# A hybrid decoder layer: five gate products moved to an earlier call, and a gate-path block moved ahead of the sparse branch's last projection

## The chip, the cores and the metric

One core of one Trainium2 chip runs the whole layer. The metric is the device time of one execution in microseconds, the median of several. Of the engines, PE (TensorE) multiplies matrices, ACT (ScalarE) and DVE (VectorE) work elementwise, POOL (GpSimd) does a few special operations, and SP issues most of the transfers between memory and the chip.

## The reference

The layer mixes three branches over 1024 tokens of width 1024. All matrix products are in fp32.

```python
h = rms_norm(x, g_norm)
proj = h @ w_in                     # 1024 x 7912, split into the parts below
(q_a, k_a, v_a, q_i, k_i, w_i, z_a, c_q, c_kv, k_rope, z_b, q_m, z_m, gate_logits) = split(proj)
q_a = partial_rope(rms_norm(q_a), ...)              # the same for k_a, 8 heads of 64
o_a = dsa_attention(q_a, k_a, v_a, q_i, k_i, w_i)   # sparse: 256 keys a query, chosen by an indexer
o_b = causal_attention(q_b, k_b, v_b)               # dense: q_b, k_b, v_b from c_q, c_kv, k_rope
o_m = cross_attention(q_m, mem)                     # 4 heads, 256 memory tokens
ys = [o_a * silu(z_a), o_b * silu(z_b), o_m * silu(z_m)]
branch = [ys[n] @ w_branch[n] for n in range(3)]
out = x + sum(sigmoid(gate_logits[n]) * branch[n] for n in range(3)) @ w_out
```

## The kernel before

**Products.** An fp32 product is three matmuls (`mm3`, lines 273 to 275): the high half of one side by the high half of the other, high by low, low by high. `wsplit` (line 239) makes the halves of a weight tile: ACT casts the raw tile to the high half (line 240), DVE subtracts it from the raw tile for the low half (line 243). `wload` (line 245) takes a raw buffer, has SP load it (line 257), and splits it. The halves of h, transposed, stay in hTh and hTl all the time.

**Stages.** The norm and the memory branch come first (to 240 us), then the dense branch with its eight heads (to 520), then the indexer (to 680). From 680 to 1023 the outputs of the memory and the dense branch are projected, and in between come the sparse branch's own projections: `qkv(p)` for the four pairs of heads p = 0 to 3, and `z_early(0, w)` for blocks w of the sparse branch's gate path z_a. The sparse attention itself (1023 to 1240) and the last projections (to 1400) follow. In the background of 680 to 1002 DVE and ACT search each row's 256th largest index score by bisection (tiles kd.. and ka.., `run_topk`); what is left of it runs between the other work.

**Fillers.** The gate products (tiles f, weights f_.., results fo) are independent of everything else in a stage; `Filler.run(n)` hands out n of them, three matmuls of 512 columns each. `attention()` (line 530) calls it at four places ahead of its loop, with the four numbers of the tuple: for the dense branch `PREB`, after the first pair's keys and values have been made (`pre[0]`, line 544), after the next load is taken up (`pre[1]`), after the key transposes `k_prep` (`pre[2]`; tile bkt, line 963) and after the queries (`pre[3]`, line 550).

**The order.** The kernel is written in program order, and a list scheduler then orders the instructions of each engine by what is ready. Each engine works through its list in order; a wait at its head holds all behind it. Tiles of one tag share a ring of buffers, and a tile waits until the one whose buffer it takes has been read for the last time.

**Around the change.** `qkv(p)` loads four weight tiles of 384 columns (a{p}w0 to a{p}w3, three transfers each) and then makes eight blocks of 128 tokens, 24 matmuls of 384 columns each. ACT copies each block out of the accumulator (line 1398); after each four blocks come the squares (line 1405), sums (line 1406), POOL's power (line 233), the rotary embedding (lines 422 to 427) and the scaling (lines 1420 to 1423). `scaled` for the second four blocks is kept back in `behind` until the next `catch_up()`. `z_early(0, w)` loads two weight tiles (in the trace z0w_0r and z0w_4r, 256 KB each, for every w) and makes 48 matmuls of 512 columns (tile z); its results go through line 1269 on ACT and line 1270 on DVE to memory. The raw tiles of qkv and of z share a ring of two buffers (`pool_raw = [2, 8, 768]`, line 1201), their halves rings of eight and seven. `NZG = 3`: the blocks w = 0, 1, 2 are made early, the fourth later. In the text z_1 and z_2 are the blocks w = 1 and w = 2, z2_0 and z2_4 the two weight tiles of z_2, and a_0, a_1 the first and the second four blocks of a qkv; r, h and l at a name's end are the raw tile, the high and the low half.

Of the kernel before, what the change touches and what calls it, by code (L numbers as in the profile page):

```python
# [34 lines left out]
WSM = [1]  # L35
WSB = [1]
WSI = [1]
PREB = (0, 0, 0, 16)
PREA = (0, 0, 4, 4)
NFQ = 2  # L40
PFQ = 4
NZG = 3
# [57 lines left out]
def hybrid_kernel(  # L100
# [296 lines left out]
    def pool_filler(pool, jobs, bufs, banks):  # L397
        return Filler(half_loader(pool, bufs), lambda nm: pool.tile([P, 512], F32, tag="fo", name=nm, bufs=1), jobs, banks)

    def take_jobs(n, cnt):  # L400
        r = all_jobs[n][:cnt]
        del all_jobs[n][:cnt]
        return r
# [432 lines left out]
    with ExitStack() as ph:  # L836
# [176 lines left out]
        fp = ph.enter_context(tc.tile_pool(name="bfill", bufs=1, reuse_waits="tile"))  # L1013
        attention(kv_gen, k_prep, q_prep, scores, pv, pool_filler(fp, take_jobs("G", NFB), FW, FBB), PFB, PREB, GENB, LDJ)

# [260 lines left out]
    def z_early(n, w, zc, wpool, wk, bg, loaded=None):  # L1276
        get = z_part(n, w, zc, wpool, wk, loaded=loaded)
        for j in range(2):
            sz = get(j)
            nc.gpsimd.dma_start(s_z[w * P:(w + 1) * P, j * 512:(j + 1) * 512], sz)  # L1280
            bg(zi[0], 5.1)
        z_done.add((n, w))
# [52 lines left out]
    with w3s as ph:  # L1335
# [10 lines left out]
        def catch_up():  # L1346

            while behind:
                behind.pop()()
# [89 lines left out]
        def load_q(p, hh):  # L1439
            qs = st["q", p, hh] = hd.tile([P, NT, P], FR, tag="qs", name=f"aqs{p}_{hh}")  # L1440
            for j in range(2):
                nc.sync.dma_start(f(qs)[:, 4 * j:4 * j + 4, :],
                                  s_qa[p][j].rearrange("p (t h d) -> p t h d", t=4, h=2)[:, :, hh, :])
# [3 lines left out]
        def early(a, b):  # L1447
            for w in range(a, b):
                z_early(0, w, C_ZA, wpool, wk, run_topk)
                catch_up()  # L1450
# [5 lines left out]
        ys.close()  # L1456
        fp = hds.enter_context(tc.tile_pool(name="afill", bufs=1, side="right", reuse_waits="tile"))
        hd = hds.enter_context(tc.tile_pool(name="aheads", bufs=2, side="right", reuse_waits="tile"))
        early(1, 2)
        a3 = qkv(3)  # L1460
        with tc.issue_after(a3.ins):
            load_k(0)
            load_q(0, 0)
            load_q(0, 1)
        early(2, NZG)

    run_topk(None, 99)
    wkind[:] = [None, None]
# [188 lines left out]
```

## Time and profile before

| | |
|---|---|
| median of 3 runs | 1402.6 us (1394.78 to 1403.1) |
| profiled execution, its own time | 1402.0 us |
| its span in the trace | 1400.2 us |
| mean granted clock of PE | 0.994 of full speed |
| PE busy | 1358.3 us, 97% of the span |
| DVE busy | 957.9 us, 68% |
| ACT busy | 693.4 us, 50% |
| POOL busy | 213.7 us, 15% |
| share of PE in the chain of work that ended last | 67% |

Busy time says how full an engine is, not what the end waits for; where PE is as full as here, its idle stretches and what released it from them are to be looked for one by one. Times inside the trace count from the start of the span.

### The profile page before, as it was taken

What the parts mean: (1) busy time and instruction counts of PE and PEld (TensorE: products, weight loads), DVE (VectorE), ACT (ScalarE), POOL (GpSimd) and SP (SyncE); (2) the same over time, 40 slices, a digit from 0 to 9 for tenths busy, and PEclk for the clock granted to TensorE, in tenths of its full rate; (3) what the DMA queues carried; (4) which work ended last, traced back from release to release, by engine and by line L of the source; (5) the groups of instructions that cost most, each with busy time, mean ns of one, the idle gap of its engine ahead of it and who ended that gap; (6) DMA issues with size and microseconds to landing.
All of it is one profiled execution on the core that took longest, in us unless ns stands there. A gap on an engine that the chain in (4) does not pass through costs nothing.

```text
span 1400.2 us, 20838 instructions
## 1 busy us (share of the span) xinstructions
PE 1358.3 (97%) x7440; PEld 1167.8 (83%) x7440; DVE 957.9 (68%) x2346; ACT 693.4 (50%) x1520; POOL 213.7 (15%) x240
## 2 busy tenths in 40 slices
PE   7999999999999999999999999998999999999998
PEld 5998888878889888977898889788988888877787
DVE  5935445678888871388887777877768888858511
ACT  6635433256666652265665566443346666543200
POOL 3051003611101000000004102414220000004200
PEclk9999999999999999999999999999999999999999
DMA  7411222321111213011424741975351442267621
GB/s 248 141 46 53 78 62 69 108 82 38 57 50 38 64 44 114 15 39 37 131 74 167 239 113 47 224 167 146 111 182 52 129 136 54 69 195 232 197 98 67
DMA packets 154711, 147.45 MB, mean 105 GB/s; under 512 B 38000, under 2 KB 114800, under 8 KB 154608
## 3 DMA queue, kind: packets, MB, share of 16 engines
q1 hardware_dynamic: 147024, 123.58, 29.6%
q0 software_dynamic: 7008, 20.45, 4.9%
q10 hardware_dynamic: 576, 2.10, 0.4%
q8 instruction: 58, 0.95, 0.3%
q14 instruction: 45, 0.37, 0.1%
HBM read 99.43 MB, written 46.66 MB: 104 GB/s over the span
## 4 chain that ended last, share of the span: by engine, by line
PE 67%; DVE 13%; ACT 6%; DMA 4%; issue 4%; POOL 3%; SPq 1%; DVEq 0%; ACTq 0%; POOLq 0%
PE f L273 6%; PE f L274 5%; PE f L275 5%; DVE kdj L1039 3%; PE o L275 2%; PE o L273 2%; PE o L274 2%; PE br L273 2%; PE br L275 2%; PE br L274 2%; ACT kag L1045 2%; DVE idx L1233 1%; PE ixps L274 1%; PE ixps L275 1%; PE ixps L273 1%
## 5 line engine op out<-in xcount | busy, mean ns | idle before, releaser
L1045 ACT ACTIVATE kag<-idx,kaT 128x896 bf16<-128x896 f32 (+2 forms) x96 | 83.0, 865 | 43.5 <-DVE kaT L1066 34.2
L1039 DVE TENSOR_SCALAR_CACHE_REDUCE kdj<-idx,kdT 128x1024 bf16<-128x1024 f32 (+2 forms) x96 | 92.5, 964 | 1.1
L273 PE MATMUL f<-hTh,f_0h 128*128 128x512 f32 x184 | 78.8, 428 | 1.9 <-ACT fo L365 1.3
L273 PE MATMUL f<-hTh,f_1h 128*128 128x512 f32 x184 | 76.3, 415 | 0.0
L274 PE MATMUL f<-hTl,f_1h 128*128 128x512 f32 x184 | 74.4, 404 | 0.0
L275 PE MATMUL f<-hTh,f_0l 128*128 128x512 f32 x184 | 74.1, 403 | 0.0
L275 PE MATMUL f<-hTh,f_1l 128*128 128x512 f32 x184 | 73.9, 402 | 0.0
L274 PE MATMUL f<-hTl,f_0h 128*128 128x512 f32 x184 | 73.5, 400 | 0.0
L1588 POOL TENSOR_TENSOR ac<-ac,tg 128x512 f32<-128x512 f32 x16 | 24.1, 1520 | 257.6 <-DVE tg L1586 250.7
L1627 DVE TENSOR_TENSOR xr<-o,xr 128x512 f32<-128x512 f32 x16 | 11.1, 691 | 62.4 <-PE o L275 62.3
L365 ACT ACTIVATE fo<-f 128x512 f32<-128x512 f32 x48 | 28.8, 600 | 38.5 <-PE f L275 34.6
L1227 ACT ACTIVATE irl<-is 128x512 f32<-128x512 f32 (+1 forms) x80 | 37.8, 527 | 15.6 <-DVE idx L1233 11.9
L1233 DVE SCALAR_TENSOR_TENSOR idx<-irl,wi,idx 128x1024 f32<-128x1024 f32 (+5 forms) x42 | 40.3, 960 | 2.5 <-ACT irl L1227 0.8
L273 PEld LDWEIGHTS f<-hTh,f_0h 128*128 128x128 f32 x184 | 34.9, 190 | 8.2 <-ACT fo L365 3.1
L275 PEld LDWEIGHTS f<-hTh,f_0l 128*128 128x128 f32 x184 | 34.9, 190 | 6.8
L275 PEld LDWEIGHTS f<-hTh,f_1l 128*128 128x128 f32 x184 | 34.8, 189 | 6.0
L274 PEld LDWEIGHTS f<-hTl,f_1h 128*128 128x128 f32 x184 | 34.9, 190 | 4.3
L273 PEld LDWEIGHTS f<-hTh,f_1h 128*128 128x128 f32 x184 | 34.8, 189 | 4.1
L274 PEld LDWEIGHTS f<-hTl,f_0h 128*128 128x128 f32 x184 | 35.1, 191 | 3.6
L1225 PE MATMUL is<-kih,iqT 128*128 128x512 f32 (+1 forms) x80 | 30.1, 381 | 2.7 <-ACT irl L1227 2.4
L1174 DVE TENSOR_SCALAR wi<-ixps 128x8 f32<-128x8 f32 x8 | 1.3, 167 | 42.0 <-ACT xi L1172 42.0
L1226 PE MATMUL is<-kil,iqT 128*128 128x512 f32 (+1 forms) x80 | 27.5, 354 | 0.0
(1246 smaller groups left out, 4767.8 us busy)
## 6 DMA issues: line engine op xcount, KB each, us to landing
s_tg<-fo SPq DMA_DIRECT2D x48, 256.0 KB, 2.1
tg<-s_tg SPq DMA_DIRECT2D x48, 256.0 KB, 4.6
f_0r<-in_w_in_dram SPq DMA_DIRECT2D x23, 256.0 KB, 3.0
f_1r<-in_w_in_dram SPq DMA_DIRECT2D x23, 256.0 KB, 3.0
xx<-in_x_dram SPq DMA_DIRECT2D x8, 512.0 KB, 6.9
osb<-s_o SPq DMA_DIRECT2D x16, 256.0 KB, 3.4
s_acc<-ab POOLq DMA_DIRECT2D x16, 256.0 KB, 5.0
s_acc<-am POOLq DMA_DIRECT2D x16, 256.0 KB, 6.4
```

Source lines behind the costliest of these rows:

```text
L273: nc.tensor.matmul(ps, ah, bh, start=start, stop=False)
L274: nc.tensor.matmul(ps, ah, bl, start=False, stop=False)
L275: nc.tensor.matmul(ps, al, bh, start=False, stop=stop)
L365: nc.scalar.activation(o, ps, AF.Tanh, scale=0.5)
L1039: nc.vector.tensor_scalar(out=junk, in0=idx[t], scalar1=T[:, i:i + 1], scalar2=0.0, op0=ALU.is_ge, op1=ALU.add, accum_out=cnt[:, i:i + 1])
L1045: nc.scalar.activation(junk, idx[t], AF.Sign, bias=T[:, i:i + 1], accum_out=cnt[:, i:i + 1])
L1225: nc.tensor.matmul(sp[:, 0:w], q_, kih[:, k0:k0 + w], start=True, stop=False)
L1226: nc.tensor.matmul(sp[:, 0:w], q_, kil[:, k0:k0 + w], start=False, stop=True)
L1227: nc.scalar.activation(rl[:, k0:k0 + m], sp[:, 0:m], AF.Relu)
L1233: i_ = nc.vector.scalar_tensor_tensor(out=acc[:, 0:n], in0=rl[:, 0:n], scalar=wc, in1=acc[:, 0:n], op0=ALU.mult, op1=ALU.add)
L1588: nc.gpsimd.tensor_tensor(ac, ac, tg, op=ALU.add)
L1627: nc.vector.tensor_tensor(xr, ps, xr, op=ALU.add)
```

## The change

Two edits. The first moves numbers within the tuple that sets how many gate products go where ahead of the dense branch's loop: of the sixteen after the queries, five are asked for ahead of the key transposes. The second makes z_2 ahead of `qkv(3)` instead of behind it, so that nothing of the gate path lies between `qkv(3)` and the sparse attention; in its old place only `catch_up()` remains, which emits the scaling of the last four blocks.

```diff
-PREB = (0, 0, 0, 16)
+PREB = (0, 5, 0, 11)
...
-        early(1, 2)
+        early(1, NZG)
         a3 = qkv(3)
         with tc.issue_after(a3.ins):
             load_k(0)
             load_q(0, 0)
             load_q(0, 1)
-        early(2, NZG)
+        catch_up()
```

PE ahead of the dense branch's first key transposes, in the program as built. f_5_0 is the gate product in question, kv the keys and values of the first pair; the transposes (bkt) follow some twenty rows later.

```order
 L274 MATMUL kv_4_2965<-ukv0l,ckvh_1951 128x256
 L275 MATMUL kv_4_2965<-ukv0h,ckvl_1952 128x256
-L273 MATMUL f_5_0_3067<-hTh_0_142,f_5_1h 128x512
-L274 MATMUL f_5_0_3067<-hTl_0_158,f_5_1h 128x512
-L275 MATMUL f_5_0_3067<-hTh_0_142,f_5_1l 128x512
+L273 MATMUL f_5_0_3042<-hTh_0_142,f_5_1h 128x512
+L274 MATMUL f_5_0_3042<-hTl_0_158,f_5_1h 128x512
+L275 MATMUL f_5_0_3042<-hTh_0_142,f_5_1l 128x512
 L273 MATMUL kv_6_2993<-ukv0h,ckvh_1949 128x256
 L274 MATMUL kv_6_2993<-ukv0l,ckvh_1949 128x256
```

The three last matmuls of f_5_0 stand where they stood; the buffer has another number. The same holds for the other 21 of that product and for all instructions of the other engines up to the second edit.

SP, from z_1's two weight tiles on. The two added rows are z_2's; they were issued before behind the sparse attention's first keys and queries (akd, aqs).

```order
 L257 DMA z0w_0r<-in_w_in_dram 128x4x128
 L257 DMA z0w_4r<-in_w_in_dram 128x4x128
+L257 DMA z0w_0r<-in_w_in_dram 128x4x128
+L257 DMA z0w_4r<-in_w_in_dram 128x4x128
 L257 DMA a3w0r<-in_w_in_dram 128x2x128 x3
 L257 DMA a3w1r<-in_w_in_dram 128x2x128 x3
 L257 DMA a3w2r<-in_w_in_dram 128x2x128 x3
 L257 DMA a3w3r<-in_w_in_dram 128x2x128 x3
```

z_2's tiles now stand ahead of the four weight tiles of qkv(3), and the ring's two buffers go round in that order: a3w0 waits for z_2's first low half, a3w1 for a3w0's, a3w2 for a3w1's, and a3w3 for z_2's second.

DVE, behind the scaling of qkv(2)'s second four blocks (a_1qs), about 978 us in the trace before. idx, kdi, kdc and kds are top-k.

```order
 L1423 TENSOR_TENSOR a_1qs<-a_1xq,a_1qs 128x8x64
 L1114 TENSOR_SCALAR idx_6264<-kae_10461 128x896
-L243 TENSOR_TENSOR a3w3l<-a3w3r,a3w3h 128x768
+L243 TENSOR_TENSOR z0w_4l<-z0w_4r,z0w_4h 128x512
 L1074 TENSOR_SCALAR kdi_10501,kdc<-kds_10499 128x768
 L1116 TENSOR_TENSOR idx_6264<-idx_6264,cmask 128x128
```

Where the low half of qkv(3)'s fourth weight tile stood, there stands now that of z_2's second. z_2's first low half went up to the place behind z_1's second, ahead of the block sz and the next top-k row (kdj); a3w1's and a3w2's went down one and two places. On PE the 48 matmuls of z_2 stand between z_1 and qkv(3), and behind qkv(3) both blocks of the first gate job, 48 matmuls, come ahead of the first scores S, where one block with 24 stood.

## Rows read from the trace of the kernel before

**Rows 1.** The page, busy time of PE: us, share of the span, instructions.

```profile
PE 1358.3 (97%) x7440; PEld 1167.8 (83%) x7440; DVE 957.9 (68%) x2346; ACT 693.4 (50%) x1520; POOL 213.7 (15%) x240
```

**Rows 2.** Waits of PE, whole span: who waits <- for whom: total us, times, longest.

```profile
PE a L274 <- DVE a3w3l L243: 4.3, 1, 4.3
PE bkt L963 <- POOL xk L948: 2.5, 1, 2.5
...
PE f L273 <- ACT fo L365: 1.3, 3, 0.6
```

**Rows 3.** PE in order of time: start us, us, line, operation, out<-in, [idle before <-releaser].

```profile
960.60 0.40 PE L273 MATMUL z<-hTh,z0w_0h 128*128 128x512 f32 x1
...
971.57 0.39 PE L275 MATMUL z<-hTh,z0w_4l 128*128 128x512 f32 x1
971.80 0.34 PE L273 MATMUL a<-a3w0h,hTh 128*128 128x384 f32 x1
...
974.97 0.34 PE L273 MATMUL a<-a3w3h,hTh 128*128 128x384 f32 x1
979.57 0.69 PE L274 MATMUL a<-a3w3l,hTh 128*128 128x384 f32 x1 [4.27 <-DVE a3w3l L243]
...
983.90 0.47 PE L275 MATMUL a<-a3w1h,hTl 128*128 128x384 f32 x1
```

**Rows 4.** Stretches: us, PE busy, PEld, DVE, ACT, POOL, granted clock, DMA share, GB/s.

```profile
980.00:982.00 2.00, 2.00 (x8) 2.00 (x8) 2.00 (x7) 0.00 (x0) 0.25 (x1) 0.50 1.13 400
...
1030.00:1240.00 210.00, 205.89 (x1270) 175.06 (x1269) 173.18 (x493) 130.06 (x286) 0.00 (x0) 1.00 0.35 100
```

**Rows 5.** SP in order of time: weight loads issued before qkv(3).

```profile
925.25 0.37 SPq L257 DMA_DIRECT2D z0w_0r<-in_w_in_dram  x1
930.01 0.37 SPq L257 DMA_DIRECT2D z0w_4r<-in_w_in_dram  x1
932.14 1.39 SPq L257 DMA_DIRECT2D a3w0r<-in_w_in_dram  x3
...
964.86 1.39 SPq L257 DMA_DIRECT2D a3w2r<-in_w_in_dram  x3
```

**Rows 6.** ACT in order of time: casts that make the high halves.

```profile
930.77 0.62 ACT L240 CAST z0w_0h<-z0w_0r 128x512 fp32r<-128x512 f32 x1 [1.86 <-DMA z0w_0r<-in_w_in_dram]
...
933.01 0.62 ACT L240 CAST z0w_4h<-z0w_4r 128x512 fp32r<-128x512 f32 x1 [1.12 <-DMA z0w_4r<-in_w_in_dram]
...
968.55 0.84 ACT L240 CAST a3w2h<-a3w2r 128x768 fp32r<-128x768 f32 x1 [4.75 <-DMA a3w2r<-in_w_in_dram]
```

**Rows 7.** DVE in order of time: low halves, top-k and the last rows of qkv(2).

```profile
933.66 0.69 DVE L243 TENSOR_TENSOR z0w_4l<-z0w_4r,z0w_4h 128x512 fp32r<-128x512 f32 x1
...
934.87 0.61 DVE L1039 TENSOR_SCALAR_CACHE_REDUCE kdj<-idx,kdT 128x384 bf16<-128x384 f32 x1
...
963.89 0.93 DVE L243 TENSOR_TENSOR a3w0l<-a3w0r,a3w0h 128x768 fp32r<-128x768 f32 x1
...
969.95 0.69 DVE L1406 TENSOR_REDUCE a_1ss<-a_1sq 128x8 f32<-128x512 f32 x1 [2.19 <-ACT a_1sq L1405]
...
977.67 0.68 DVE L1423 TENSOR_TENSOR a_1qs<-a_1xq,a_1qs 128x512 fp32r<-128x512 f32 x1
...
978.57 0.95 DVE L243 TENSOR_TENSOR a3w3l<-a3w3r,a3w3h 128x768 fp32r<-128x768 f32 x1
```

**Rows 8.** PE (z, f, S), then DVE, in order of time at the head of the sparse attention.

```profile
1012.11 0.39 PE L273 MATMUL z<-hTh,z0w_0h 128*128 128x512 f32 x1
...
1023.27 0.39 PE L273 MATMUL f<-hTh,f_0h 128*128 128x512 f32 x1
...
1029.95 0.40 PE L1537 MATMUL a_3S<-akh,a_3qT 128*128 128x512 f32 x1
...
1023.29 0.69 DVE L1423 TENSOR_TENSOR a_1qs<-a_1xq,a_1qs 128x512 fp32r<-128x512 f32 x1 [1.83 <-ACT a_1qs L1422]
...
1025.23 1.29 DVE L1496 TENSOR_TENSOR akl<-akt,akh 128x512 fp32r<-128x512 f32 x2 [0.44 <-ACT akh L1495]
```

## The prediction

> **What bounds the kernel now.** I read the page first: PE is busy for 1358.3 of the 1400.2 us [rows 1], so the whole kernel is one queue of matmuls, and a change that only moves matmuls can win or lose no more than idle time and half-clock time of PE, 42 us in all. Then the table of PE's waits, longest first: it names where those us lie. Two of its rows bear on this change [rows 2]: the 4.3 us in which qkv(3), the last projection of the sparse branch, waits for the low half of its fourth weight tile (a3w3l), and the 2.5 us in which the first key transposes of the dense branch (bkt) wait for POOL's xk. The third row is a small wait for the eviction of a gate product, used below. Then PE in order of time around 972 us [rows 3]: z_1's 48 matmuls of 512 columns run 0.233 us apart (960.60 to 971.57), qkv(3) starts at 971.80 with 0.176 us a matmul, and its 20th matmul starts at 979.57 instead of 975.15. So 4.42 us are lost there. Behind it the clock is at its lower level: the granted clock is 0.50 in 980 to 982 [rows 4], and 14 matmuls from 979.57 to 983.90 take 4.33 us for 13 steps that cost 2.29 at 0.176: 2.04 us more. This stall costs 6.46 us in all.
>
> **Edit 1, the five gate products ahead of the key transposes: 0 us.** The tuple moves five of the sixteen steps to an earlier call, but the scheduler already had the products of that job ahead of the transposes. In the programs as built the instructions of PE, DVE, ACT, POOL and SP stand in the same order with the same waits until the second edit begins; only buffer numbers differ. What this edit might have covered, the 2.5 us before bkt [rows 2], stays.
>
> **Edit 2, z_2 ahead of qkv(3).** What it takes away: qkv(3) starts 48 x 0.233 = 11.2 us later on PE, so a3w3l, late by 4.4 us, is no longer what ends last. That is -6.46 us.
>
> What it adds is a new wait of the same kind. The raw weight ring has two buffers. Before, SP used them after z_1's two tiles (issues at 925.25 and 930.01) for a3w0 at 932.14 and a3w1, and the third, a3w2r, could go only at 964.86, when a3w0l had been made [rows 5]. Now z_2's two tiles take those two places. Their high halves are soon made on ACT, but the low half of the second, z2_4l, stands in DVE's order where a3w3l stood: behind a_1qs and one top-k row. That is the row at 978.57 [rows 7], long after the data has landed. PE needs it at the 15th matmul of z_2 (k = 4, the L275 product): 971.80 + 14 x 0.233 = 975.07.
>
> When is it made? First z2_0: issued at 932.14, where a3w0r was. z_1's tiles needed 5.5 us (925.25 to the cast at 930.77) and 3.0 us (930.01 to 933.01) to land [rows 5, 6]. I take 3.0, since the like of it has one transfer of this size just ahead of it and nothing large behind, and keep 5.5 as the upper bound. It lands at 935.1; by the steps of z_1's second tile the low half starts 0.65 us after the cast (933.01 to 933.66) and the next top-k row 1.21 us after that (933.66 to 934.87). So the top-k row that started at 934.87 starts at 935.14 + 0.65 + 1.21 = 937.0: DVE is 2.1 us late. From there DVE is full, then hands its results to POOL's power (a_0rr), ACT and back, in order, so the 2.1 us stay in the chain until a3w0l (963.89, now about 966.0). Behind that hangs SP's next issue (a3w1r now, in a3w2r's place), its landing 3.7 us later (964.86 to 968.55), ACT's cast, and behind that cast in ACT's order the square a_1sq, hence DVE's a_1ss (969.95), the power on POOL, a_1qs (977.67) [rows 5 to 7]. All of it 2.1 us late, so z2_4l starts at about 980.7; it has 512 columns, 0.69 us as z_1's [rows 7], and PE starts at 981.4. Lost: 981.4 - 975.07 = 6.3 us, and the half clock behind it as before, 2.04: +8.4 us. Bounds: with no lateness at all (some idle time of DVE swallows it) the loss is 4.2 + 2.0 = 6.2; with the landing of 5.5 us, 8.9 + 2.0 = 10.9.
>
> The Trainium skill (SBUF — State Buffer, "The DMA setup-cost knee") puts a transfer at about 2 us plus its bytes over 436 GB/s, so 2.6 us for these 256 KB. By that estimate DVE would be 1.7 us late instead of 2.1, and the sum would come out 0.4 us lower. The trace shows 3.0 and 5.5 for the same tile, and the sum goes by the trace.
>
> Is there a second stall at a3's own weights? a3w1r to a3w3r now go out one by one, each when a low half is done; a3w3r last, behind z2_4l at 981.4. With 3.7 us to land and the cast and low half behind top-k rows it is there by about 989. PE has 34 matmuls of z_2 left (7.9 us, and 2 for the half clock), so qkv(3) starts at 991.3 and wants a3w3l 3.3 us later. No stall; 5 us to spare. The loads behind it on SP (keys, queries, f_0's weights) are wanted after 1023, 40 us later.
>
> **The head of the sparse attention.** Before, z_2 lay between qkv(3)'s end (1012.11) and the gate products, and covered the normalisation of the last rows: a_1qs came 11.2 us after that end, the scores S 17.8 us after it [rows 8]. Now S of the first unit comes behind 48 gate matmuls, 16 key transposes and the queries: 11.2 us and about twice the 1.1 us that they took between 1023.27 and 1029.95, so 13.4 us behind qkv(3). The query copy on DVE stands behind a_1qs, two more akl (0.65 each), a weight split and takes 0.4: about 13.0. It just fits. Two small prices remain: the second gate block waits for the eviction of the first, at most the 0.6 us of such a wait [rows 2], I take 0.4; and 24 matmuls of filler (5.6 us) that used to lie under S and softmax are spent earlier, in a stretch that has only 4.1 us of idle PE in 210 [rows 4] and meets the old order again at the fifth gate job: 0 to 2 us, I take 0.3, since more gate products stand ready behind.
>
> **Sum.** -6.46 + 8.4 + 0.4 + 0.3 = +2.6 us on the profiled execution's 1402.0 us: 1404.6. That execution lies 0.6 us below the median of the runs (1402.6), so the forecast, rounded down for that z_1's gate on ACT no longer stands behind a late cast, is 1404.5.
>
> **Rivals.**
> (a) The stall goes away: z2_4l is made before 975.07. For it: ACT has the high half by about 938, and the data lies there for 40 us. Against it: DVE works in order, and what stands ahead needs the last rows of qkv(2), whose matmuls end at 960.60; even with no lateness the chain puts z2_4l at 978.6. Price: -6.46 + 0.7 = -5.8, 1396.
> (b) z_2's first tile lands as slowly as z_1's first, 5.5 us: DVE is 4.6 us late, the loss at this place 10.9 instead of 8.4, and the time 1407.
> (c) The other side, slower: the head of the sparse attention starves. The query copy waits for a chain through ACT, DVE and POOL that z_2 no longer covers; it has about 0.4 us to spare. Each us that it is later is a us of idle PE, and past some us the half clock adds 2 more: 2 to 8 us late gives 1407 to 1415. It is over 1% only if the chain is about 10 us later than I reckon; nothing in the rows is that long.
> (d) Edit 1 acts after all and takes bkt's wait away with its half clock: -2.5 - 2.0, so 1400 with the rest. Against it stands the identical order.
>
> **How the numbers follow.** Forecast (1402 to 1407) 0.62; (b) 0.13; (a) 0.10; (c) 0.09; (d) 0.03; something unseen 0.03. The range 1397 to 1410 leaves out (a), half of (c) and the unseen: 0.17. A measurement of this kernel can tell about 1% from no change (its three runs lie 0.6% apart). All that the edits touch, 6.5 us at one stall and 4.5 at the other, is under 1%, so faster has 0.01; slower needs the far end of (c): 0.03; within 1%: 0.96.
>
> **What would show it.** In the waits of PE after: no row for a3w3l; in its place z, L275, for z's second low half, about 6 us; bkt unchanged at 2.5; half clock from about 981 to 985 among z_2's matmuls. The DVE row of that low half directly behind a_1qs and idx at about 980.7, and the low half of z_2's first tile near 935.8. A wait of S or of a query transpose in the first unit under 1 us. I am wrong if z's second low half is made much earlier or PE waits for a3's weights too, and the sum is then off by the us in those two rows.

## The result and the profile after

The changed kernel takes 1409.3 us (1407.3 to 1411.2) beside 1400.8 us of the kernel before on the same chip (1394.8 to 1403.1): a ratio of 1.0063, with a 95% interval of 1.0046 to 1.0081. It is slower by 8.5 us, under 1%, where +2.6 was forecast. The time lies above the forecast's own range of 1402 to 1407 and 0.7 us inside the outer one, 1397 to 1410. The profiled execution took 1409.46 us (span 1407.7), 7.5 more than that of before.

Busy times on the page, as in [rows 1]:

```profile
PE 1360.6 (97%) x7440; PEld 1167.8 (83%) x7440; DVE 956.4 (68%) x2346; ACT 692.4 (49%) x1520; POOL 214.8 (15%) x240
```

The same work, 2.3 us more busy time of PE (matmuls at half clock count as busy) and 5 us more of idle time. PE's waits, longest first, as in [rows 2] (total us, times, longest):

```profile
PE z L275 <- DVE z0w_4l L243: 6.6, 1, 6.6
...
PE f L273 <- ACT fo L365: 2.8, 5, 0.9
...
PE a_2pt L462 <- DVE a_2p L519: 2.5, 2, 2.0
PE bkt L963 <- POOL xk L948: 2.5, 1, 2.5
```

The row for a3w3l is gone and a row for z_2's second low half stands in its place, 6.6 us long (6.3 were forecast). bkt waits as before. But there is a wait that the prediction did not have: a transpose of the attention's probabilities (a_2pt) waits 2.0 us for DVE, where the same row of the kernel before had 0.4 at most:

```profile
PE a_2pt L462 <- DVE a_2p L519: 0.9, 2, 0.4
```

PE at the first of these places, as in [rows 3], and the stretches around it, as in [rows 4] (the seventh figure, just ahead of the last two, is the granted clock):

```profile
971.78 0.39 PE L273 MATMUL z<-hTh,z0w_0h 128*128 128x512 f32 x1
...
974.81 0.40 PE L274 MATMUL z<-hTl,z0w_4h 128*128 128x512 f32 x1
981.85 0.80 PE L275 MATMUL z<-hTh,z0w_4l 128*128 128x512 f32 x1 [6.64 <-DVE z0w_4l L243]
982.44 0.63 PE L273 MATMUL z<-hTh,z0w_4h 128*128 128x512 f32 x1
...
986.71 0.48 PE L274 MATMUL z<-hTl,z0w_0h 128*128 128x512 f32 x1
```

```profile
978.00:980.00 2.00, 0.00 (x0) 0.00 (x0) 0.00 (x0) 0.45 (x1) 1.97 (x3) 1.00 0.35 131
980.00:982.00 2.00, 0.15 (x1) 0.15 (x1) 1.80 (x4) 2.00 (x4) 0.58 (x2) 0.52 0.35 131
...
984.00:986.00 2.00, 2.00 (x6) 1.52 (x6) 2.00 (x2) 0.00 (x0) 0.54 (x1) 0.50 0.93 269
...
988.00:990.00 2.00, 2.00 (x10) 1.65 (x9) 1.21 (x2) 1.75 (x3) 0.00 (x0) 1.00 0.88 184
...
1030.00:1240.00 210.00, 203.86 (x1230) 171.31 (x1228) 169.29 (x496) 124.05 (x274) 7.54 (x13) 0.99 0.35 101
```

z_2's 15th matmul was due at 974.81 + 0.23 = 975.04 and started at 981.85: 6.8 us. The ten steps from 982.44 to 986.71 have 0.427 us each where they want 0.233: granted clock 0.50, the lower level of 1.2 GHz; with the slower steps at either end that is 2.4 us. The last line is the other half of the result: of 210 us in the sparse attention PE is now idle 6.1, where it was 4.1 [rows 4].

Why z0w_4l came when it came: SP, ACT and DVE in order of time, as in [rows 5 to 7].

```profile
931.06 0.37 SPq L257 DMA_DIRECT2D z0w_0r<-in_w_in_dram  x1
934.38 0.37 SPq L257 DMA_DIRECT2D z0w_4r<-in_w_in_dram  x1
935.96 1.39 SPq L257 DMA_DIRECT2D a3w0r<-in_w_in_dram  x3
966.43 1.39 SPq L257 DMA_DIRECT2D a3w1r<-in_w_in_dram  x3
```

```profile
934.59 0.62 ACT L240 CAST z0w_0h<-z0w_0r 128x512 fp32r<-128x512 f32 x1 [0.97 <-DMA z0w_0r<-in_w_in_dram]
...
937.25 0.62 ACT L240 CAST z0w_4h<-z0w_4r 128x512 fp32r<-128x512 f32 x1 [1.54 <-DMA z0w_4r<-in_w_in_dram]
```

```profile
965.47 0.93 DVE L243 TENSOR_TENSOR a3w0l<-a3w0r,a3w0h 128x768 fp32r<-128x768 f32 x1
...
971.46 0.69 DVE L1406 TENSOR_REDUCE a_1ss<-a_1sq 128x8 f32<-128x512 f32 x1 [2.99 <-ACT a_1sq L1405]
...
980.20 0.69 DVE L1423 TENSOR_TENSOR a_1qs<-a_1xq,a_1qs 128x512 fp32r<-128x512 f32 x1 [2.39 <-ACT a_1qs L1422]
980.81 0.39 DVE L1114 TENSOR_SCALAR idx<-kae 128x896 bf16<-128x896 bf16 x1
981.11 0.68 DVE L243 TENSOR_TENSOR z0w_4l<-z0w_4r,z0w_4h 128x512 fp32r<-128x512 f32 x1
```

The tile is in SBUF and its high half is being made at 937.25. Its low half stands on DVE behind a_1qs and idx, as the order said, at 981.11: 44 us later. a3w0l is 1.6 us later than before (2.1 were forecast); a_1qs, with a wait for ACT of its own, is 2.5 later.

The head of the sparse attention, as in [rows 8]: the first scores on PE, and the copy of their queries on DVE.

```profile
1039.59 0.40 PE L275 MATMUL f<-hTh,f_1l 128*128 128x512 f32 x1
1039.82 0.40 PE L1537 MATMUL a_3S<-akh,a_3qT 128*128 128x512 f32 x1
```

```profile
1038.10 0.68 DVE L243 TENSOR_TENSOR f_1l<-f_1r,f_1h 128x512 fp32r<-128x512 f32 x1
1038.70 0.42 DVE L1523 CAST a_3qT<-a_3q 128x256 fp32r<-128x256 f32 x1
```

The queries are there 0.7 us ahead of S; S waits for nothing. What is lost is lost behind it. From the last score of the tile a_2 to the transpose of its probabilities, DVE and ACT need nearly the same time in both kernels: 1122.31 to 1126.87 before, 1130.66 to 1135.53 after. Before, 12 gate matmuls lie in between on PE (the last at 1126.45); after, 6, and then nothing is left that is ready. The kernel before, then the kernel after, PE in order of time:

```profile
1122.31 0.28 PE L1538 MATMUL a_2S<-akl,a_2qT 128*128 128x256 f32 x1
...
1126.45 0.39 PE L275 MATMUL f<-hTh,f_1l 128*128 128x512 f32 x1
1126.87 0.41 PE L462 MATMUL a_2pt<-ident,a_2p 128*128 128x128 f32 x2
```

```profile
1130.66 0.28 PE L1538 MATMUL a_2S<-akl,a_2qT 128*128 128x256 f32 x1
...
1133.11 0.40 PE L1538 MATMUL a_1S<-akl,a_1qT 128*128 128x512 f32 x1
1135.53 0.41 PE L462 MATMUL a_2pt<-ident,a_2p 128*128 128x128 f32 x2 [2.03 <-DVE a_2p L519]
...
1138.19 0.63 PE L275 MATMUL f<-hTh,f_0l 128*128 128x512 f32 x1
```

Behind this wait, too, the granted clock is at its lower level for a while:

```profile
1137.00:1139.00 2.00, 2.00 (x8) 1.50 (x7) 1.64 (x3) 1.20 (x3) 0.00 (x0) 0.52 0.46 165
1139.00:1141.00 2.00, 2.00 (x13) 1.96 (x12) 0.12 (x1) 0.00 (x0) 0.00 (x0) 0.63 0.00 0
```

**Where the time went, by stretches.** PE's timeline is cut at the 96 score products (line 1538). "Lost" is the length of a stretch less its matmuls at their usual step (median distance to the next: 0.23 us for 512 columns, 0.17 for 384, 0.12 for 256, 0.083 for 128), so it holds waits, half clock and the small gaps at each change of work. For z_1 to qkv(3) the steps are those of [rows 3]. The steps are rounded, so an entry holds to a few tenths. "1st to 16th" goes from the first score product to the start of the 17th, and so on by sixteens; "to last" ends where the 96th starts, and the last column where the last matmul starts. In the text the head is everything from the end of qkv(3) to the end of "to 48th". In brackets stands the number of gate matmuls f in the stretch. Before and after come first, the experiments of the next section below them.

| kernel | z_1 to end of qkv(3) | to 1st score | 1st to 16th | to 32nd | to 48th | to last | behind it, whole length |
|---|---|---|---|---|---|---|---|
| before | 6.6 | 0.5 (24) | 2.4 (54) | 4.2 (58) | 4.4 (62) | 9.6 (156) | 166.7 (30) |
| after | 9.3 | 1.2 (48) | 3.3 (49) | 5.2 (49) | 8.5 (53) | 9.5 (155) | 164.6 (30) |
| e1_preb | 7.5 | 0.4 (24) | 2.4 (54) | 4.1 (58) | 4.3 (62) | 9.5 (156) | 164.3 (30) |
| e2_z | 6.7 | 1.2 (48) | 3.4 (49) | 5.2 (49) | 8.4 (53) | 9.2 (155) | 163.2 (30) |
| e3_wz8 | 0.0 | 1.2 (48) | 3.5 (49) | 5.3 (49) | 7.0 (53) | 9.6 (155) | 160.7 (30) |
| e5_z3 | 7.9 | 1.1 (24) | 2.5 (54) | 4.2 (58) | 4.4 (62) | 9.6 (156) | 163.1 (30) |
| e10_late | 0.8 | 5.8 (24) | 2.3 (54) | 4.2 (58) | 4.4 (62) | 9.4 (156) | 164.1 (30) |
| e11_late_after | 1.8 | 1.9 (48) | 3.5 (49) | 5.3 (49) | 8.5 (53) | 9.5 (155) | 160.2 (30) |
| e12_prea | 7.5 | 0.9 (48) | 2.7 (54) | 4.8 (57) | 3.7 (61) | 9.4 (158) | 162.3 (6) |
| e16_prea_after | 8.6 | 1.4 (51) | 4.3 (53) | 4.7 (55) | 3.9 (61) | 9.4 (158) | 162.4 (6) |
| e18_66 | 4.2 | 1.2 (48) | 3.9 (49) | 5.4 (50) | 3.3 (63) | 9.7 (156) | 162.3 (18) |

After against before: +2.7 up to the end of qkv(3), +6.7 from there to the 48th score, nothing from there to the last, -2.1 behind it; 7.3 of the 7.5. The -2.1 is not the change's: e1_preb has before's order there, and took 164.3. Of the +2.7, too, a part is the spread of single executions: up to the end of qkv(3) the kernels with before's order lose 6.6, 7.5 and 7.5 (before, e1_preb, e12_prea), those with the changed kernel's 9.3, 6.7 and 8.6 (after, e2_z, e16_prea_after), in the mean 1.0 apart. The head loses as good as the same in executions of one order: 11.5 and 11.2 us in before and e1_preb, 18.2 in both after and e2_z.

### The profile page after: what moved, and what is told of

The parts are those of the page before. It is cut to its first block, busy times and chain, and to the rows that moved or that the text cites. A ratio compares the mean times of both kernels' runs of the same rounds, so it can differ in the third digit from the quotient of the medians.

```text
span 1407.7 us, 20841 instructions
## 1 busy us (share of the span) xinstructions
PE 1360.6 (97%) x7440; PEld 1167.8 (83%) x7440; DVE 956.4 (68%) x2346; ACT 692.4 (49%) x1520; POOL 214.8 (15%) x240
## 4 chain that ended last, share of the span: by engine, by line
PE 71%; DVE 11%; DMA 6%; ACT 5%; issue 4%; POOL 2%; SPq 1%; DVEq 0%; ACTq 0%; POOLq 0%
PE f L273 6%; PE f L274 6%; PE f L275 6%; PE o L275 2%; PE o L273 2%; PE o L274 2%; DVE kdj L1039 2%; PE a L273 2%; PE z L275 2%; PE a L274 2%; PE a L275 2%; PE z L273 2%; PE z L274 2%; PE br L273 1%; PE br L274 1%
## 5 line engine op out<-in xcount | busy, mean ns | idle before, releaser
L1627 DVE TENSOR_TENSOR xr<-o,xr 128x512 f32<-128x512 f32 x16 | 11.1, 691 | 59.7 <-PE o L275 59.7
L273 PEld LDWEIGHTS f<-hTh,f_0h 128*128 128x128 f32 x184 | 35.1, 191 | 11.1 <-ACT fo L365 5.8
```

The costliest lines, as they stand in the source:

```text
L273: nc.tensor.matmul(ps, ah, bh, start=start, stop=False)
L1627: nc.vector.tensor_tensor(xr, ps, xr, op=ALU.add)
```

## The experiments

Medians in us, each with that of the kernel before beside it on the same chip:

| kernel | median | before | ratio (95%) |
|---|---|---|---|
| e1_preb | 1398.6 | 1398.4 | 1.0006 (0.9995 to 1.0017) |
| e2_z | 1406.7 | 1398.4 | 1.0062 (1.0045 to 1.0079) |
| e3_wz8 | 1405.8 | 1398.4 | 1.0055 (1.0041 to 1.0069) |
| e5_z3 | 1412.3 | 1398.4 | 1.0096 (1.0081 to 1.0112) |
| e10_late | 1396.8 | 1398.1 | 0.9992 (0.9977 to 1.0006) |
| e11_late_after | 1401.1 | 1398.1 | 1.0017 (1.0002 to 1.0032) |
| e12_prea | 1405.8 | 1398.1 | 1.0049 (1.0030 to 1.0069) |
| e3c_tg2 | 1417.5 | 1398.1 | 1.0134 (1.0115 to 1.0154) |
| e13_bank | 1400.6 | 1402.0 | 0.9994 (0.9978 to 1.0009) |
| e15_bank_only | 1400.9 | 1402.0 | 0.9995 (0.9981 to 1.0008) |
| e16_prea_after | 1408.3 | 1399.0 | 1.0068 (1.0055 to 1.0080) |
| e18_66 | 1399.8 | 1399.0 | 1.0001 (0.9989 to 1.0012) |

### Which of the two edits: e1_preb and e2_z

e1_preb is the kernel before with the first edit alone, e2_z with the second alone.

```diff
-PREB = (0, 0, 0, 16)
+PREB = (0, 5, 0, 11)
```

> The kernel before with the first edit alone, the tuple (0, 5, 0, 11); z_2 stays behind qkv(3). Theory: the first edit changes nothing, since the instructions stand in the same order on every engine; the time is that of before within 2 us, and PE's wait of bkt for xk stays near 2.5 us. Rival (the first edit acts): the time differs by more than 2 us, with bkt's wait gone for a gain, or with another wait in the dense branch's head for a loss, and part of the 8.5 us that the changed kernel lost belongs here.

> The kernel before with the second edit alone: z_2 ahead of qkv(3), the tuple as it was. Theory: the whole loss of the changed kernel comes from here, so before + 8.5 us (7 to 10), with the wait of z for z's second low half near 6.6 us and the first heads of the sparse attention as in the changed kernel. Rival (the first edit acts): less than before + 6.

The first edit: no difference (+0.3 us), bkt's wait unchanged at 2.5. The second: +8.3, all of it. In the head of the attention the profile of e2_z has the same waits as the changed kernel's, down to a_2pt's 2.0; the wait in z_2 is shorter in this execution, 5.0 us instead of 6.6.

### The stall at z_2 alone: e3_wz8 and its control e3c_tg2

The halves of z's weights share a ring of seven buffers. z_2's second low half is the eighth of z_1's and z_2's, and takes the buffer that z_1's last block still reads until about 969. That is why it was put so late on DVE; the prediction had seen only the place. e3_wz8 gives the ring an eighth buffer; to make room the last projections get two buffers for transposed gates instead of three, which e3c_tg2 does alone.

```diff
-                    wkind[:] = [("wz", 7, 512)] * 2
+                    wkind[:] = [("wz", 8, 512)] * 2
...
-    def branch(n, zc, wpool, wk, yp, o_T, emit, bg=None, tgb=3, wkt=None, zb=2, ob=2, mid=None):
+    def branch(n, zc, wpool, wk, yp, o_T, emit, bg=None, tgb=2, wkt=None, zb=2, ob=2, mid=None):
```

> The changed kernel with eight buffers instead of seven for the halves of z's weight tiles (the last projections have two transposed-gate buffers instead of three, to make room). z_2's second low half is the eighth half of z_1 and z_2, so it no longer has to wait until z_1's first high half has been read for the last time; in the instruction order it now stands right behind z_2's first low half, some 40 us earlier. Theory (two separate losses): the wait of 6.6 us in z_2 and the half clock behind it, 2.4 us, go, 9 us in all, and the 7 us that the first heads of the sparse attention lose because their gate products were spent ahead of the scores stay: changed kernel - 9, about before - 1. Rival 1 (one loss: the attention's head starts badly because the projection ahead of it ran late): the 7 us go too, changed kernel - 16, about before - 7. Rival 2 (the wait only moves to a3's weights or to the scaling behind qkv(3)): changed kernel - 2 or less.

> The changed kernel with two transposed-gate buffers instead of three in the last projections: what had to be given up in e3_wz8 to make room for the eighth half buffer, and nothing else. If those buffers explain why e3_wz8 came out only about as slow as the changed kernel although its stall was gone: changed kernel + 8 to + 10, with waits of br and z for DVE's am (line 1366) between 880 and 925 us. If they cost nothing: the changed kernel's own time, and the eighth buffer itself cost what the stall gave back.

DVE in e3_wz8 makes the low half at once, and PE's waits of e3_wz8 have no row for it:

```profile
939.15 0.69 DVE L243 TENSOR_TENSOR z0w_4l<-z0w_4r,z0w_4h 128x512 fp32r<-128x512 f32 x1 [1.76 <-ACT z0w_4h L240]
```

```profile
PE br L273 <- DVE am L1366: 3.7, 3, 2.1
...
PE z L273 <- DVE am L1366: 3.2, 1, 3.2
PE f L273 <- ACT fo L365: 2.8, 5, 0.9
PE a_2pt L462 <- DVE a_2p L519: 2.5, 2, 2.0
```

The loss up to the end of qkv(3) goes from 9.3 to 0.0, but the time comes out only 1 us under the changed kernel's. The missing third gate buffer takes the rest: e3c_tg2 lies 19 us above before, 11 above the changed kernel, and its z_1 starts 9.8 us later (970.3 against 960.6; 968.2 in e3_wz8), behind waits of PE for am and ab in the branches' projections (4.2 and 2.4 us in all). Against this control the eighth buffer brings 12 us, of which 9.6 are the stall (e3c_tg2 lost 9.6 there). The head of the attention still loses 17.0 of 18.2 us, so it is a loss of its own and does not follow from the stall ahead of it; rival 1 falls.

### The stall by DVE's order: e11_late_after and e10_late

No buffer is changed here. The scaling of qkv(2)'s second four blocks is emitted inside qkv(3) instead of ahead of it, so on DVE the weight half goes ahead of a_1qs. e11_late_after does it in the changed kernel, e10_late in the kernel before (there for w = 1 alone).

```diff
                 z_early(0, w, C_ZA, wpool, wk, run_topk)
-                catch_up()
+                if w == 0:
+                    catch_up()
```

> The changed kernel with the same move of the scaling of qkv(2)'s second four blocks into qkv(3). z_2's second low half goes up five rows on DVE, behind kae (975.53 + 1.1 in the trace of the changed kernel). Theory: its wait on PE falls from 6.6 to about 2.3 us and the half clock behind it shrinks: changed kernel - 4 to - 7, so about before + 3; the first heads of the sparse attention lose their 7 us as before this move. Rival 1 (the attention's head loses because of the stall ahead of it): the head's loss shrinks with the stall, changed kernel - 8 or more.

> The kernel before, with one thing moved: the scaling of qkv(2)'s second four blocks (a_1xk, a_1qs) is emitted not behind z_1 but inside qkv(3), behind its second block. On DVE the fourth weight tile's low half a3w3l thereby goes up four rows, ahead of that scaling, directly behind the top-k row kae (974.62 + 1.1 in the trace before); every other order stays. Theory (a weight half that has landed waits for its turn in DVE's order, and PE waits with it): a3w3l starts near 975.7 instead of 978.57, PE's wait falls from 4.3 to about 1.4 us, and the half clock behind it shrinks or goes: before - 3 to - 5. Rival (the tile's landing and cast, 972.4 to 973.2, or the scaling itself set the stall): before within 1 us.

In e11_late_after the wait is 1.5 us, the loss at this place falls from 9.3 to 1.8, and the time is about 6 us below the changed kernel's (1.0017 against 1.0062 of e2_z, whose order is the changed kernel's). PE's wait:

```profile
PE z L275 <- DVE z0w_4l L243: 1.5, 1, 1.5
```

The head loses as much as ever (19.2). So of 8.3 us some 6 can be had back by emitting the scaling later, which puts the weight half four rows up on DVE, directly behind kae.

In e10_late the same move takes away the stall of the kernel before, 4.3 us to 0.5, and next to nothing comes of it (-1.3; the interval holds 0). PE's waits of e10_late:

```profile
PE f L273 <- DVE sz L1270: 3.5, 1, 3.5
```

qkv(3) ends 5.8 us earlier behind z_1, and then PE waits at the first gate product for an accumulator that DVE has not read, with half clock behind it (granted clock 0.50 in 1024 to 1026). The expectation of -3 to -5 missed that.

### Is it the accumulator? e13_bank and e15_bank_only

e13_bank is e10_late with z_2's two halves in other accumulators; e15_bank_only has this shift without the moved scaling.

```diff
+        turn[0] += 1
         early(2, NZG)
+        turn[0] -= 1
```

> e10_late, where the stall at a3w3l was gone but PE then waited 3.5 us at the first gate product for the accumulator that z_2's first half had filled and DVE's sz (line 1270) had not yet read. Here z_2's two halves take the next two accumulators of the three that z goes round, so the first gate product finds its own free; the instruction order of every engine is the same. Theory (that wait was one accumulator's, and qkv(3)'s 5 us are then kept): the wait of f for sz goes with its half clock, the scores come some 3.5 us earlier than in e10_late, and the time is before - 4 to - 6. Rival (the head of the sparse attention is bound by the scaling chain through ACT, DVE and POOL, whatever PE does): PE waits as long for the query copy instead, and the time is that of e10_late, before - 1.

> The kernel before with the accumulator shift of e13_bank alone, without the moved scaling. Both theories: before within 1 us, since the kernel before has no wait of f for sz; if it is faster by 3 us or more, e13_bank's gain is not from a3w3l.

The wait only goes elsewhere. PE's waits of e13_bank:

```profile
PE z L273 <- ACT a_1xv L1398: 5.4, 1, 5.4
```

ACT of e13_bank in order of time:

```profile
1013.94 0.62 ACT L1422 CAST a_0qs<-a_0xq 128x512 fp32r<-128x512 f32 x1 [7.07 <-POOL a_0xq L1420]
1014.47 0.26 ACT L1398 COPY a_1xq<-a 128x128 f32<-128x128 f32 x1
```

Now z_2 itself waits, for ACT to evict qkv(3)'s last blocks (line 1398). These stand on ACT behind the cast a_0qs, and that waits 7.1 us for POOL's a_0xq. The time is that of before. e15_bank_only lies level with before as well (0.9995), so the shift by itself does nothing. So the rival holds, though PE waits for an accumulator and not for the query copy that it named: in the kernel before, the chain through ACT, DVE and POOL sets when the attention can begin, and the stall at a3w3l lay beside it. From the first matmul of z_1 to the first score it is 69.4, 70.2 and 70.1 us with the stall (before, e1_preb, e15_bank_only) and 68.9 and 70.7 without it (e10_late, e13_bank).

What that chain hangs on is in the traces too. It begins on DVE with the sums of qkv(3)'s first four blocks (a_0ss), and these stand behind top-k rows. DVE of before, then of e10_late, in order of time:

```profile
1001.95 0.23 DVE L1116 TENSOR_TENSOR idx<-idx,cmask 128x128 bf16<-128x128 bf16 x1
1002.10 0.68 DVE L1406 TENSOR_REDUCE a_0ss<-a_0sq 128x8 f32<-128x512 f32 x1
```

```profile
1003.36 0.22 DVE L1116 TENSOR_TENSOR idx<-idx,cmask 128x128 bf16<-128x128 bf16 x1
1003.50 0.68 DVE L1406 TENSOR_REDUCE a_0ss<-a_0sq 128x8 f32<-128x512 f32 x1
```

In all five kernels a_0ss starts 41.1 to 41.8 us after z_1's first matmul, with no idle time of DVE ahead of it, and the cast a_0qs on ACT waits the same 7.1 us for POOL and starts at 50.0 to 50.7. The stall of PE doesn't move them. So a stall that the rows price at 6.46 us was worth about 1 us in that kernel, and the intervals of both experiments hold 0.

### z_2's old place filled again: e5_z3

Four blocks are made early instead of three: z_1 and z_2 ahead of qkv(3), z_3 behind it.

```diff
-NZG = 3
+NZG = 4
...
-        early(1, NZG)
+        early(1, 3)
...
-        catch_up()
+        early(3, NZG)
```

> The changed kernel (z_2 ahead of qkv(3)) with the fourth gate-path block, z_3, made behind qkv(3), in the place that z_2 had before; the last projections then load z_3 instead of making it, so that PE's work is the same in all. Theory: the wait of z for z's second low half (6.6 us, and 2.4 us of half clock) stays, and the sparse attention's first scores come again behind 24 gate matmuls, so its 7 us go: before + 1 to + 4. Rival 1 (the attention's head loses because the stall ahead of it came late): the 7 us stay, before + 8. Rival 3 (z_2's place itself, not the spent gate products, costs): before + 8 as well, but with the loss ahead of the attention.

The head's loss is gone (12.2 up to the 48th score, before 11.5, after 18.2), with the stall in z_2 still there (6.1). But the time is the worst but one, because z_3 had been the cover of another wait, at the start of the last projections. PE's waits of e5_z3:

```profile
PE br L273 <- ACT yh L1309: 10.0, 2, 9.7
PE z L275 <- DVE z0w_4l L243: 6.1, 1, 6.1
```

The stretch behind the last score is 163.1 us without z_3's 11.2: about 11 more than the others' 163.4 (mean of those with 30) for the same work. The mechanism is confirmed at its place; the forecast of the sum (+1 to +4) missed what z_3 had hidden.

### The gate products: e12_prea, e16_prea_after, e18_66

The order before the scores is not the tuple's alone: with z_2 gone the scheduler puts 48 gate matmuls there, though the tuple asks for 24. What the tuple sets is the stock: by the table's brackets 354 gate matmuls lie ahead of the last score in every kernel with (0, 0, 4, 4), 366 with (0, 0, 6, 6) and 378 with (0, 0, 8, 8), wherever z_2 stands.

```diff
-PREA = (0, 0, 4, 4)
+PREA = (0, 0, 8, 8)
```

> The kernel before, z_2 behind qkv(3) as it was, but the sparse attention's tuple asks for 8 and 8 gate products ahead of its loop instead of 4 and 4, so that 48 gate matmuls lie ahead of the first scores instead of 24, as in the changed kernel. The work is the same in all. Theory (gate products spent ahead of the scores are missed under the first softmaxes): before + 4 to + 7, with a wait of a_2pt for a_2p of about 2 us and the half clock behind it, and the stall at a3w3l unchanged. Rival (the head's loss in the changed kernel comes from z_2's absence there: late scaling, late keys and queries): before within 1 us.

> The changed kernel with 8 and 8 gate products asked for ahead of the sparse attention's loop instead of 4 and 4. In the order as built the gate matmuls stand so, counted ahead of the first score matmul and then between every 16th of the 96: 51, 53, 55, 61, 50, 58, and behind the last score 6; in the changed kernel they stood 48, 49, 49, 53, 49, 55, and 30. Theory (what the head of the sparse attention loses is the gate matmuls missing between the first 48 scores): the matmuls' lost time between qkv(3) and the 48th score goes back to that of the kernel before, 6 us less than in the changed kernel, and a_2pt's wait of 2 us goes; behind the last score some 3.5 us are lost instead, as in e12_prea, where 24 gate matmuls less lay there too; in sum changed kernel - 1 to - 4, and the wait in z_2 stays. Rival (the head loses because z_2 doesn't cover the scaling of the last rows, whatever the gate matmuls do): its loss stays, and the time is the changed kernel's + 2 to + 4.

> e11_late_after (the changed kernel, with the scaling of qkv(2)'s second four blocks moved into qkv(3)) with 6 and 6 gate products asked for ahead of the loop instead of 4 and 4: counted as in e16_prea_after, 48, 49, 50, 63, 48, 57 and behind the last score 18. Theory: the ten more between the 32nd and the 48th score take away a_2pt's wait of 2 us with the half clock behind it, some 3 to 4 us, and the tail gives back 1 to 2: e11_late_after - 1 to - 3, about the kernel before. Rival (the tail is worth as much as the head): the time of e11_late_after within 1 us.

e12_prea, the kernel before with this tuple, came out at +7.7 us (4.2 to 9.6 by the interval), as large as expected, but not where: its head loses 12.1 us, like that of before. The tuple had handed out 24 gate matmuls more, so 172 still lay between the 1st and the 48th score. They are missing at the other end, where 6 instead of 30 lie behind the last score: that stretch takes 162.3 us with 24 x 0.23 = 5.5 us less of work, against 160 to 167 in the kernels with 30 (mean 163.4). By the mean that is 4.4 us lost there; PE's longest wait of br for yh is 2.3 us, where it was 1.0 in before. Where the rest of the 7.7 us lies these traces do not show.

e16_prea_after, the changed kernel with this tuple, turns the head back: a_2pt's wait is gone, the head loses 14.3 instead of 18.2. Another wait stands at its start:

```profile
PE z L275 <- DVE z0w_4l L243: 6.5, 1, 6.5
...
PE a_3S L1537 <- DVE a_3mx L490: 1.8, 1, 1.8
```

And the tail pays for the 24 matmuls: in all +9.3, within 1 us of the changed kernel. The expected -1 to -4 did not come: the head gave 3.9 instead of 6, and the tail took at least as much.

e18_66, e11_late_after with (0, 0, 6, 6), puts ten of them where a_2pt waited: that stretch loses 3.3 instead of 8.5, and the time is 0.7 us above before, 2.2 below e11_late_after by the ratios, whose intervals overlap. It is level with the kernel before; no version here beats it clear of noise.

Between the 1st and the 48th score, over all kernels of the table: 174 gate matmuls (before, e1, e5, e10) go with 10.8 to 11.1 us lost, 172 (e12) with 11.2, 169 (e16) with 12.9, 162 (e18) with 12.6, 151 (after, e2, e3, e11) with 15.8 to 17.3. Loss follows their number, if not strictly (e18_66 with 162 loses 0.3 less than e16_prea_after with 169), whether the stall in z_2 is there or not, and whether z_2 stands behind qkv(3) or not.

## Why the prediction was right and where it failed

That the measured time lies inside the outer range is owed to that range's width and not to the sum: +2.6 was forecast and +8.5 came, a miss of 6 us, nearly all of it in one term.

- **Edit 1 = 0.** Right: e1_preb.
- **-6.46, the stall at a3w3l goes.** Right in the changed kernel: no row is left, and z_1 to the end of qkv(3) lost 6.6 before. e10_late adds that this was no 6 us to be gained in the kernel before.
- **+8.4, the new stall at z_2's 15th matmul.** Right in place, in releaser and nearly in size: 6.8 + 2.4 = 9.2 in the profiled execution, while e2_z, with the same order, loses 6.7 there. z2_0 landed in 3.5 us, where 3.0 was taken, but SP issued it at 931.06, not 932.14; so DVE was 1.6 us late instead of 2.1, and its wait for ACT's a_1qs (2.39) made it 2.5. The cause behind DVE's order, the ring of seven halves, was not seen. The Trainium skill (SBUF — State Buffer, "The DMA setup-cost knee") would give 2.6 us for these 256 KB, an estimate by its fit; the rows show 3.5 here, so the trace stands.
- **No stall at a3's own weights.** Right: no such row. **fo, 0.4.** The row rose from 1.3 to 2.8, but the waits ahead of the first score are 0.25; the others are part of the next point.
- **"24 matmuls of filler ... are spent earlier ... 0 to 2 us, I take 0.3, since more gate products stand ready behind."** This step failed: between the 1st and the 48th score 17.0 us are lost where 11.0 were, so +6.0 (with the 0.7 ahead of the first score that makes the 6.7 of the head). No more stand ready: between the 1st and the 48th score the program hands out a fixed number, and those pulled ahead of the scores are missing there, 151 instead of 174. And the bound was wrong in kind. The 4.1 us of idle PE in 210 [rows 4] were idle time with the cover in place; they say nothing of the idle time once the cover is taken. The prediction's first paragraph has the same fault, where it lets a change that moves matmuls "win or lose no more than" 42 us of idle and half-clock time: that bounds a gain and no loss, and the 42 us are idle time alone, since matmuls at half clock count as busy. For this term, an estimate from the rows would have been the work taken out, 23 x 0.23 = 5.3 us, plus the half clock behind a wait (2.0 at the stall that was known).
- **Rivals.** (c) had the right stretch and sign, and the wrong wait: the query copy was ready 0.7 us early, at 1038.70, 12.8 us behind the end of qkv(3) (13.0 forecast). PE starved, but 96 us later, at a softmax. (a), (b) and (d) did not happen.

What stays open: how the 6.7 us of the head divide between waits, half clock and the small gaps when work changes. Between the 1st and the 48th score the rows give 2.5 more of waits of 0.2 us and over (4.0 against 1.5), and about 1.7 for the half clock at 1137 to 1141 (2 us at 0.52 and 2 at 0.63); the rest is spread over gaps that have no releaser. Open is also where the loss of e12_prea lies beyond the 4.4 us at its end.

## What to carry to other kernels

Independent work that a scheduler may pull forward is a fixed stock. When a block that covered a chain is moved away, the stock fills the hole, and the loss appears later, where the stock would have been: count it stretch by stretch in both orders, and price the missing matmuls in full. Idle time measured under a cover bounds nothing once the cover is gone. And before a stall is counted as gain, look whether another engine's chain ends at the same place; taking away the wait of one then only shows the wait of the other.

## What was not expected of the hardware

The granted clock fell late, and not each time: after the wait of 2.0 us at a_2pt PE resumed at 1135.53, the stretch 1135 to 1137 still shows 1.00, and it is 1137 to 1139 that shows 0.52. In e3_wz8 the same wait (2.02 us, PE resumed at 1133.91) left 1.00 throughout 1129 to 1141, and that stretch of the table lost 7.0 us instead of 8.5. In e11_late_after the wait of 1.5 us in z_2 left no such stretch (1.00 throughout 974 to 988). And the stretch behind the last score took from 160.2 to 166.7 us in executions with the same matmuls in it, so a single profile is 3 us uncertain there.
